# A hybrid decoder layer on one core: per-row roots and more products on TensorE in the opening, and a residual that the storing transfers add

## The chip, the core and the metric

The kernel runs on one core of a Trainium2 chip. Five engines work beside each other: TensorE (PE; its weight loads are listed as PEld) makes products into PSUM, VectorE (DVE), ScalarE (ACT) and GpSimd (POOL) work elementwise, and SyncE (SP) mostly issues transfers; POOL and ACT issue some as well. Every engine takes its instructions strictly in the order in which they stand in its own queue. The metric is the time of one execution in microseconds (us), lower is better; the median of three runs stands for a kernel.

## What is computed

One decoder layer on x (1024 x 1024, float32) with a conditioning vector c (1024):

```python
c_act = jax.nn.silu(c)
mod = c_act @ w_ada[l] + b_ada[l]
sh1, sc1, g1, sh2, sc2, g2 = [m[:, None, :] for m in jnp.split(mod, N_MOD, axis=-1)]
h = rmsnorm(x, pre_w_mix[l]) * (1.0 + sc1) + sh1
proj = h @ w_in[l]
...
mix = jnp.concatenate([attn, rec], axis=-1) @ w_out[l]
x = x + g1 * rmsnorm(mix, post_w_mix[l])
h = rmsnorm(x, pre_w_mlp[l]) * (1.0 + sc2) + sh2
u = jnp.square(jax.nn.relu(h @ w_up[l]))
x = x + g2 * rmsnorm(u @ w_down[l], post_w_mlp[l])
```

`rmsnorm(x, w)` divides each row by the root of its mean square plus 1e-6 and multiplies by w. The change touches the two ends: the first line of `h` (norm of x, shift `sh1`, scale `sc1`) with the first products of `h @ w_in`, and the last line, the final residual.

## The kernel before

The 1024 rows of x are eight tiles of 128 rows (`tb` 0 to 7) in two halves of four tiles (`th` 0 and 1); the 1024 columns are eight blocks of 128 (`kb` 0 to 7) and, in memory, two halves of 512 (`half`, `hf`). For precision a product is made of a high and a low part of each operand (`h`/`l` at a name's end), hence three products where the mathematics has one.

**The order** is the order of the code. From the line `pin(True, ACT, DVE, POOL, PE)` on, `Queue` keeps every instruction behind the last one on its engine, so the order in which lambdas and helpers are called is the order in the queues. All recorded operations have the one line L39, so tiles' names tell them apart.

**The opening** (about 0 to 70 us). SP loads x for tiles 0 to 3, then the weights `w_ada` of the first shift and scale as tiles `wa<gate>_<qt>_<kp>` (gate 0 is the shift, 1 the scale; `qt` is a quarter of the columns), with the weights `wqr`, `wkvr` between them. ACT squares each half row (`norm_sq`, tile `jx`). `norm_rstd(th)` takes the four rows' sums together: one POOL sum (`ssum`), one POOL `tensor_scalar` (`t_x`), one POOL power -0.5 (`r_x`). `norm_scale` multiplies x by it. `first_T` transposes a block of four x tiles on TensorE (`xT`), and `split_evac` makes of it `hhi` (ACT), `f` (POOL) and `hlo` (DVE), with the column's factors `a1`, `sh1`, `ns1`.

These factors come from the first modulation. For kb 0 and 1 (`qt` 0), `mod0_cols(e)` makes the shift as eight products of a 128x128 weight tile with a column of `cs` (silu of c), 128x1 each, while the scale's eight tiles are first summed on DVE (`mod0_acc`, tile `m`) and then reduced by one product with a column of ones. For kb 2 to 7 (`qt` 1 to 3) shift tiles are scaled on ACT and summed on POOL (`mod1_shift`), scale tiles are summed on DVE (`mod1_scale`), and `mod1_cols(qt)` reduces both by products with ones: eight for `qt` 1, four for `qt` 2 and 3, for which DVE first folds the two halves of the shift's sum (`wa<-wa`, 128x256). `mod1_finish` turns the columns into `a1`, `sh1`, `ns1` on DVE. Each float32 128x1 product stands in the trace as two records.

The loop over kb issues the products `pq` (512 wide, weights `wq`) and `pk` (256 wide, weights `wkv`) of four tiles with `hhi`, then the transpose of the next block and the modulation's columns, then the products with `hlo`.

**The middle** is not touched except for one store: `out_proj(tb)` computes x after the first sub-layer (`xr`) and stores it by a POOL transfer to a scratch array `x1d`.

**The tail.** The last group of the down projection adds products to `acc<tb>_<half>`, and a list `later` places the last norm's steps behind the products: `square` (ACT), `root` (DVE and POOL, tile `rrf`), `gated` (POOL, times the gate `gw`), `scaled` (ACT, times the root), `residual` (DVE, plus x1 loaded from `x1d` through `take()`), and a store by SP. Rows 2 and 6 end in `final`, one DVE instruction for root and residual together. `last_rows` does rows 3 and 7: the last products are `pdlx`, row 7's gated halves are `gl`, its root `l_r`; row 3 is scaled on ACT and its x1 added on POOL.

## Time and profile before

| | us |
|---|---|
| runs (three) | 1121.09, 1121.69, 1123.86 |
| median | 1121.69 |
| the profiled execution | 1118.99 |
| its span | 1117.2 |
| TensorE busy in it | 1073.3 |

The profiled execution is one more execution with its own time; its span is the time between its first and last recorded instruction, and the rest, 1.8 us, lies around it. The views read below are the page (busy times, the chain that ended last, transfers), the list of waits, the timeline of stretches, and windows of 2 us.

### The profile page before, as it was taken

The numbers are of one execution on the slowest core, as the hardware profiler recorded it, in microseconds if no ns is written. First come the engines' busy times: TensorE is split into PE (matmuls) and PEld (weight loads), VectorE is DVE, ScalarE is ACT, GpSimd is POOL, SyncE is SP. The second block draws the span as 40 slices with busy tenths as digits, with TensorE's granted clock in tenths as the row PEclk, the third lists the DMA queues.
The fourth block names the chain that finished last, engine by engine and source line by source line (L and its number), as shares of the span: only waits on it lengthen the run. The fifth ranks groups of instructions, "written<-read, shape, count | busy, mean of one in ns | idle before, by whom it ended". The sixth has DMA issues, their size and how long they took to land.

```text
span 1117.2 us, 16056 instructions
## 1 busy us (share of the span) xinstructions
PE 1073.3 (96%) x5406; PEld 878.0 (79%) x5406; DVE 817.6 (73%) x1338; ACT 593.7 (53%) x1228; POOL 404.4 (36%) x522
## 2 busy tenths in 40 slices
PE   5899999999999999999999999999999999999984
PEld 4788676788788788888888888888888888888863
DVE  4965877878865664639777766767767787998777
ACT  5645554374465664565655555556664544555343
POOL 3644211034224753422434434443333334300046
PEclk9999999999999999999999999999999999999997
DMA  9601400634310343323577676767998888987554
GB/s 354 243 11 38 133 1 22 196 97 139 126 58 1 118 156 113 115 74 121 198 247 252 230 258 230 255 216 248 324 348 297 274 287 279 334 283 244 160 179 160
DMA packets 103699, 207.30 MB, mean 186 GB/s; under 512 B 13344, under 2 KB 14000, under 8 KB 103616
## 3 DMA queue, kind: packets, MB, share of 16 engines
q1 hardware_dynamic: 89568, 161.07, 42.4%
q0 software_dynamic: 13760, 44.68, 12.0%
q8 instruction: 42, 0.69, 0.3%
q10 hardware_dynamic: 288, 0.52, 0.1%
q14 instruction: 41, 0.34, 0.1%
HBM read 151.17 MB, written 55.05 MB: 185 GB/s over the span
## 4 chain that ended last, share of the span: by engine, by line
PE 79%; DVE 7%; ACT 4%; DMA 4%; POOL 3%; issue 2%; SPq 0%; DVEq 0%; POOLq 0%; ACTq 0%
PE pua L39 14%; PE pda L39 13%; PE pdc L39 7%; PE puc L39 7%; PE po L39 6%; PE pu L39 4%; PE pdb L39 3%; PE pub L39 3%; PE pv L39 3%; PE phg L39 3%; PE phq L39 3%; PE phf L39 3%; PE pq L39 3%; DVE acc L39 2%; DMA wa<-wada 1%
## 5 line engine op out<-in xcount | busy, mean ns | idle before, releaser
L39 POOL TENSOR_TENSOR b<-b,b 128x512 f32<-128x512 f32 x64 | 90.0, 1406 | 221.7 <-DMA b<-w_dn 221.3
L39 ACT ACTIVATE s<-s 128x512 f32<-128x512 f32 x84 | 52.9, 631 | 32.5 <-DVE s L39 31.1
L39 ACT ACTIVATE dw<-dwr 128x512 fp32r<-128x512 f32 x72 | 45.3, 630 | 44.9 <-DMA dwr<-td 26.5
L39 DVE TENSOR_TENSOR dw<-dwr,dw 128x512 fp32r<-128x512 f32 x72 | 57.5, 799 | 9.0 <-ACT dw L39 8.9
L39 DVE TENSOR_TENSOR acc<-pda,acc 128x512 f32<-128x512 f32 x68 | 46.3, 682 | 12.3 <-PE pda L39 12.2
L39 POOL DMA_DIRECT2D td<-b x64 | 35.9, 561 | 19.0 <-POOL b L39 19.0
L39 DVE TENSOR_TENSOR wt<-s,wt 128x512 fp32r<-128x512 f32 x42 | 38.8, 924 | 1.2 <-ACT wt L39 1.1
L39 ACT ACTIVATE s<-pua 128x512 f32<-128x512 f32 x28 | 16.7, 596 | 39.6 <-PE pua L39 36.9
L39 ACT ACT_TABLE_LOAD x28 | 35.9, 1283 | 1.2 <-PEq L1704 0.7
L39 POOL DMA_DIRECT2D b<-w_dn x64 | 34.4, 540 | 2.6 <-issue 2.5
L39 DVE SCALAR_TENSOR_TENSOR macc<-wada,cs,macc 128x512 f32<-128x512 f32 x42 | 33.6, 799 | 2.2 <-DMA wada<-wada 1.6
L39 POOL TENSOR_TENSOR comb<-comb,rd 128x512 f32<-128x512 f32 x8 | 11.7, 1458 | 63.3 <-DVE rd L39 44.2
L39 PE MATMUL pua<-bt_0h,wt 128*128 128x512 f32 x84 | 32.7, 389 | 0.0
L39 PE MATMUL pua<-bt_1h,wt 128*128 128x512 f32 x84 | 32.7, 389 | 0.0
L39 PE MATMUL pua<-bt_2h,wt 128*128 128x512 f32 x84 | 32.7, 389 | 0.0
L39 PE MATMUL pua<-bt_3h,wt 128*128 128x512 f32 x84 | 32.7, 389 | 0.0
L39 DVE TENSOR_TENSOR wt<-a,wt 128x512 fp32r<-128x512 f32 x42 | 32.7, 777 | 0.0
L39 ACT ACTIVATE wt<-s 128x512 fp32r<-128x512 f32 x42 | 26.3, 627 | 10.1 <-DVE s L39 9.8
L39 POOL TENSOR_TENSOR acc<-acc,gw 128x512 f32<-128x512 f32 x14 | 20.2, 1454 | 30.6 <-ACT fin L39 30.6
L39 PE MATMUL pda<-dw,du_6h 128*128 128x512 f32 x96 | 29.8, 392 | 1.1 <-DVE acc L39 1.1
L39 PE MATMUL pdc<-dw,du_3h 128*128 128x512 f32 x96 | 29.7, 390 | 0.2 <-DVE acc L39 0.2
L39 DVE TENSOR_TENSOR s<-puc,s 128x512 f32<-128x512 f32 x14 | 9.7, 690 | 27.3 <-issue 25.2
(754 smaller groups left out, 3796.6 us busy)
## 6 DMA issues: line engine op xcount, KB each, us to landing
dur<-ud SPq DMA_DIRECT2D x112, 256.0 KB, 4.4
wada<-wada SPq DMA_DIRECT2D x64, 256.0 KB, 3.4
b<-w_dn POOLq DMA_DIRECT2D x64, 256.0 KB, 5.1
td<-b POOLq DMA_DIRECT2D x64, 256.0 KB, 3.3
dwr<-td SPq DMA_DIRECT2D x64, 256.0 KB, 4.2
a<-w_u SPq DMA_DIRECT2D x56, 256.0 KB, 4.5
dwr<-w_dn SPq DMA_DIRECT2D x48, 256.0 KB, 4.5
ud<-s SPq DMA_DIRECT2D x42, 256.0 KB, 3.4
```

Of the source, the lines that this page charges most:

```text
L39: ins = op(*args, **kw)
```

## The change

It has three parts.

**Opening.** (1) `norm_rstd(th, a, b)` takes rows a to b: one small DVE instruction for each row and one POOL power for the group, and is called for rows 0 and 1, then 2, then 3 as their squares are there; the factor 32 of the mean moves into `prew1s`. Rows 0 and 1 are then scaled on DVE, 2 and 3 on ACT. (2) ACT runs a sigmoid on a constant first, and silu of c comes behind the first row's squares. (3) For kb 0 and 1 the scale's tiles 4 to 7 are no longer summed on DVE but multiplied with `cs` on TensorE, four 128x1 products more in each `mod0_cols`; the scale's tile `wa1_0_0` is loaded ahead of the shift's `wa0_0_0`. (4) For `qt` 1 the last two blocks of both gates go to TensorE too, eight products more in `mod1_cols(1)`; for `qt` 3 the DVE fold is left out and `mod1_cols(3)` makes eight products where it made four. (5) Calls of `mod1_shift`, `mod1_scale`, the low part of `wq` (now `first_wql`), the second half's scaling of x and the squares of the second four tiles stand at other kb. (6) At kb 0 all `pq` products stand ahead of the `pk` products.

**Middle.** `out_proj` stores x of six of the eight row tiles straight into `out`; only rows 3 and 7 go to `x1d`.

**Tail.** For rows 0, 4, 1, 5, 2 and 6 there is no x1 load, no DVE residual and no SP store: both halves are scaled on ACT, and POOL issues two transfers which add the tile onto `out` (`onto_x`). Their second gated half is made on DVE. Rows 3 and 7 end in one DVE instruction for each half, with root and x1, and a store on SP and ACT in turn.

```diff
-    def norm_rstd(th):
-        ss = small.tile([P, 4], F32, tag="ss4", bufs=1, name=f"ssum{th}")
-        POOL.tensor_tensor(ss, ssx[th][:, :, 0], ssx[th][:, :, 1], ALU.add)
-        rx[th] = rstd_of(ss, D, 4, f"x{th}")
+    def norm_rstd(th, a, b):
+
+        if not a:
+            rx[th] = small.tile([P, 4], F32, tag="rr4", name=f"r_x{th}")
+        t = small.tile([P, 4], F32, tag="rs4", name=f"t_x{th}{a}")
+        for i in range(a, b):
+            DVE.tensor_scalar(t[:, i:i + 1], ssx[th][:, i, 0:1], ssx[th][:, i, 1:2], D * EPS, ALU.add, ALU.add)
+        POOL.tensor_tensor(rx[th][:, a:b], t[:, a:b], mhalf[:, a:b], ALU.pow)
...
         for k in range(KB):
-            wsh = wa1[0, 2 * e + k // 4, 0][:, k % 4 * P:k % 4 * P + P]
-            PE.matmul(pst[:, 0:1], lhsT=wsh, rhs=cs[:, k:k + 1], start=(k == 0), stop=(k == KB - 1))
+            PE.matmul(pst[:, 0:1], lhsT=wa0(e, k, 0), rhs=cs[:, k:k + 1], start=(k == 0), stop=(k == KB - 1))
+        for k in range(4, KB):
+            PE.matmul(pst[:, 1:2], lhsT=wa0(e, k, 1), rhs=cs[:, k:k + 1], start=(k == 4), stop=False)
         if between:
             between()
-        PE.matmul(pst[:, 1:2], lhsT=acc, rhs=ones[:, 0:1], start=True, stop=True)
+        PE.matmul(pst[:, 1:2], lhsT=acc, rhs=ones[:, 0:1], start=False, stop=True)
...
-        if kps[-1] == 3 and qt > 1:
+        if kps[-1] == 3 and qt == 2:
             w0 = wa1[qt, 0, 0]
             DVE.tensor_tensor(w0[:, 0:256], w0[:, 0:256], w0[:, 256:512], ALU.add)
...
         pst = a_ps(f"pm1_{qt}")
-        n = 2 if qt == 1 else 1
+        n = 2 if qt in (1, 3) else 1
         for j in range(4):
+            for h in range(2 if qt == 1 else 0):
+                PE.matmul(pst[:, j:j + 1], lhsT=wa1[1, 3, j // 2][:, 256 * h + (j % 2) * P:256 * h + (j % 2 + 1) * P],
+                          rhs=cs[:, 6 + h:7 + h], start=(h == 0), stop=False)
...
-            for gate in (0, 1) if qt == 0 else (1, 0):
+            for gate in (0, 1) if qt == 0 and kp % 2 else (1, 0):
...
+        if kb == 1:
+            mod1_shift(1, (1, 2))
+            mod1_scale(1, (2,))
...
         if kb == 0:
-            mod1_shift(1)
-        if kb == 1:
-            mod1_scale(1, range(2, 4))
+            mod1_shift(1, (0,))
         if kb in (2, 4):
-            mod1_shift(kb // 2 + 1, range(2, 4))
+            mod1_shift(kb // 2 + 1, range(kb - 2, 4))
             mod1_scale(kb // 2 + 1, range(2, 4))
...
-            nc.gpsimd.dma_start(x1d[tb][:, hs], xr)
+            nc.gpsimd.dma_start(x1d[tb // 4][:, hs] if tb % 4 == 3 else out[tb * P:(tb + 1) * P, hs], xr)
...
-    def residual(tb, half):
-        DVE.tensor_tensor(accs[tb][half], accs[tb][half], take(), ALU.add)
-        pend.append((out[tb * P:(tb + 1) * P, half * 512:half * 512 + 512], accs[tb][half]))
+    def onto_x(tb):
+
+        for half in range(2):
+            POOL.dma_start(out[tb * P:(tb + 1) * P, half * 512:half * 512 + 512], accs[tb][half], accum_op=ALU.add)
...
-                on(step + 2, lambda tb=tb, half=half: gated(tb, half))
-                for j, hf in ((3, 1 - half), (4, half)) if t < 2 else ():
-                    on(step + j, lambda tb=tb, hf=hf: scaled(tb, hf))
-                for j, hf in ((4, 0), (5, 1)) if t < 2 else ():
-                    on(step + j, lambda tb=tb, hf=hf: residual(tb, hf))
+                on(step + 2, lambda tb=tb, half=half: gated(tb, half, DVE))
+                for hf in (1 - half, half):
+                    on(step + 3, lambda tb=tb, hf=hf: scaled(tb, hf))
+                on(step + 4, lambda tb=tb: onto_x(tb))
...
-        final(6, 1)
-        xa = [take(), take()]
-        for half in range(2):
-            scaled(a, half)
-            POOL.tensor_tensor(accs[a][half], accs[a][half], xa[half], ALU.add)
-        for half in range(2):
-            DVE.scalar_tensor_tensor(gl[half], gl[half], one["r"][:, 0:1], take(), ALU.mult, ALU.add)
-            (nc.scalar if half else nc.sync).dma_start(out[b * P:(b + 1) * P, h[half]], gl[half])
-        store(a, 0)
-        final(6, 0)
-        store(a, 1, nc.scalar)
+        for tb, rr, src in ((a, rr_[a], accs[a]), (b, one["r"], gl)):
+            for half in range(2):
+                DVE.scalar_tensor_tensor(src[half], src[half], rr[:, 0:1], take(), ALU.mult, ALU.add)
+                (nc.scalar if half else nc.sync).dma_start(out[tb * P:(tb + 1) * P, h[half]], src[half])
```

TensorE's queue at the very start, before the change. `pm` is the bank of the first column's shift and scale, `wa_0_0` and `wa_0_1` weight tiles (quarter and block of rows, then a buffer's number, which tells the two gates apart), `m` the sum made on DVE; x4 is four 128x1 products.

```order
L39 MATMUL pm_0_265<-cs,wa_0_0_144 128x1 x4
L39 MATMUL pm_0_265<-cs,wa_0_1_148 128x1 x4
L39 MATMUL xT_0_274<-c_ident,x_0_93 128x128
L39 MATMUL xT_0_274<-c_ident,x_0_132 128x128
L39 MATMUL xT_0_274<-c_ident,x_0_136 128x128
L39 MATMUL xT_0_274<-c_ident,x_0_140 128x128
L39 MATMUL pm_0_265<-ones,m_0_254 128x1
L39 MATMUL pq_285<-wq0h,hhi_0_291 128x512
L39 MATMUL pq_285<-wq0l,hhi_0_291 128x512
L39 MATMUL pk_303<-wkv0h,hhi_0_291 128x256
L39 MATMUL pk_303<-wkv0l,hhi_0_291 128x256
```

And after the change:

```order
L39 MATMUL pm_0_270<-cs,wa_0_0_146 128x1 x4
L39 MATMUL pm_0_270<-cs,wa_0_1_148 128x1 x4
L39 MATMUL pm_0_270<-cs,wa_0_1_150 128x1 x4
L39 MATMUL xT_0_283<-c_ident,x_0_93 128x128
L39 MATMUL xT_0_283<-c_ident,x_0_132 128x128
L39 MATMUL xT_0_283<-c_ident,x_0_136 128x128
L39 MATMUL xT_0_283<-c_ident,x_0_140 128x128
L39 MATMUL pm_0_270<-ones,m_0_265 128x1
L39 MATMUL pq_294<-wq0h,hhi_0_300 128x512
L39 MATMUL pq_294<-wq0l,hhi_0_300 128x512
L39 MATMUL pq_295<-wq0h,hhi_0_300 128x512
L39 MATMUL pq_295<-wq0l,hhi_0_300 128x512
```

A third group of four products stands ahead of the transposes, and the `pk` products no longer stand behind the first two `pq` products.

GpSimd's queue at the end, before the change. `acc_0_8030` and `acc_0_8675` are the last halves of rows 2 and 6, `acc_0_8062` and `acc_1_8289` row 3, `l_r` the root of row 7.

```order
L39 TENSOR_TENSOR acc_0_8030<-acc_0_8030,gw_5216 128x512
L39 TENSOR_TENSOR rrf_10925<-ssf_10924,mhalf 128x1
L39 TENSOR_TENSOR acc_0_8675<-acc_0_8675,gw_5216 128x512
L39 TENSOR_TENSOR acc_0_8062<-acc_0_8062,gw_5216 128x512
L39 TENSOR_TENSOR rrf_10964<-ssf_10963,mhalf 128x1
L39 TENSOR_TENSOR acc_1_8289<-acc_1_8289,gw_5216 128x512
L39 TENSOR_TENSOR l_r<-l_part,mhalf 128x1
L39 TENSOR_TENSOR acc_0_8062<-acc_0_8062,x_3_0_10857 128x512
L39 TENSOR_TENSOR acc_1_8289<-acc_1_8289,x_3_1_10872 128x512
```

And after it, where `acc_0_8078` and `acc_1_8305` are row 3, and `acc_0_8691` and `acc_1_8159` row 6:

```order
L39 DMA out<-acc_0_8046 128x512
L39 DMA out<-acc_1_8263 128x512
L39 TENSOR_TENSOR rrf_10917<-ssf_10916,mhalf 128x1
L39 TENSOR_TENSOR acc_0_8078<-acc_0_8078,gw_5232 128x512
L39 TENSOR_TENSOR rrf_10950<-ssf_10949,mhalf 128x1
L39 TENSOR_TENSOR acc_1_8305<-acc_1_8305,gw_5232 128x512
L39 DMA out<-acc_0_8691 128x512
L39 DMA out<-acc_1_8159 128x512
L39 TENSOR_TENSOR l_r<-l_part,mhalf 128x1
```

The two additions of x to row 3 behind `l_r` are gone, two gated halves have moved to VectorE, and two issues of transfers onto `out` for row 6 now stand between row 3's last gated half and `l_r`.

## Rows read from the trace of the kernel before

**Rows 1.** The page: the first row is the busy time of each engine, its share of the span and its instructions; the second the chain that ended last, by engine.

```profile
PE 1073.3 (96%) x5406; PEld 878.0 (79%) x5406; DVE 817.6 (73%) x1338; ACT 593.7 (53%) x1228; POOL 404.4 (36%) x522
...
PE 79%; DVE 7%; ACT 4%; DMA 4%; POOL 3%; issue 2%; SPq 0%; DVEq 0%; POOLq 0%; ACTq 0%
```

**Rows 2.** The view of waits, first 70 us: engine and what waits, what it waits for, then us in total, times, and the longest.

```profile
PE pm L39 <- DMA wa<-wada: 10.7, 1, 10.7
...
PE pm L39 <- DVE hlo L39: 1.7, 1, 1.7
...
PE pk L39 <- POOL wkv0l L39: 0.6, 1, 0.6
```

**Rows 3.** The timeline, 9.5 to 19.6 us: start us, us, engine, line, operation, out<-in, count, and in brackets the idle time before it and what ended that. A row with a count spans all of its instructions.

```profile
10.68 3.55 PE L39 MATMUL pm<-cs,wa 128*128 128x1 f32 x16 [10.68 <-DMA wa<-wada]
...
11.37 0.28 DVE L39 TENSOR_SCALAR m<-wa,cs 128x128 f32<-128x128 f32 x1 [6.38 <-DMA wa<-wada]
...
14.09 1.09 PE L39 MATMUL xT<-c_ident,x 128*128 128x128 f32 x4
...
16.85 0.79 PE L39 MATMUL pq<-wq0h,hhi 128*128 128x512 f32 x1 [1.30 <-ACT hhi L39]
```

**Rows 4.** The timeline of TensorE, 19.2 to 38.6 us, columns as in rows 3.

```profile
19.70 0.63 PE L39 MATMUL pq<-wq0l,hhi 128*128 128x512 f32 x1
...
23.96 2.23 PE L39 MATMUL pm<-cs,wa 128*128 128x1 f32 x16
...
29.23 0.40 PE L39 MATMUL pq<-wq1h,hhi 128*128 128x512 f32 x1
...
31.06 0.95 PE L39 MATMUL pm<-ones,wa 128*128 128x1 f32 x8
32.89 1.23 PE L39 MATMUL pm<-ones,m 128*128 128x1 f32 x8 [0.88 <-DVE m L39]
...
37.12 0.63 PE L39 MATMUL pq<-wq2h,hhi 128*128 128x512 f32 x1
```

**Rows 5.** The windows of the stretch 22 to 40 us, 2 us each, of which three are shown: the stretch, its length, busy time (and instructions) of PE, PEld, DVE, ACT and POOL, the granted clock of TensorE, the DMA share, GB/s.

```profile
34.00:36.00 2.00, 2.00 (x11) 1.77 (x11) 1.74 (x8) 1.37 (x3) 0.50 (x1) 0.75 1.05 396
36.00:38.00 2.00, 2.00 (x8) 1.61 (x7) 2.00 (x3) 1.52 (x4) 1.58 (x2) 0.50 1.06 406
38.00:40.00 2.00, 2.00 (x13) 1.82 (x12) 2.00 (x2) 0.00 (x0) 1.76 (x2) 0.90 1.04 391
```

**Rows 6.** The timeline, 44 to 57 us, columns as in rows 3.

```profile
44.92 0.60 PE L39 MATMUL pm<-ones,wa 128*128 128x1 f32 x4
...
45.39 0.58 PE L39 MATMUL pm<-ones,m 128*128 128x1 f32 x4
...
53.73 1.50 DVE L39 TENSOR_TENSOR wa<-wa 128x256 f32<-128x256 f32 x1
...
55.95 0.60 PE L39 MATMUL pm<-ones,wa 128*128 128x1 f32 x4 [1.74 <-DVE hlo L39]
```

**Rows 7.** The view of waits of TensorE, 1050 to 1104 us, columns as in rows 2.

```profile
PE pda L39 <- DVE acc L39: 2.6, 4, 1.2
```

**Rows 8.** The timeline of VectorE, 1089 to 1097.5 us, columns as in rows 3: two of the eight residual additions.

```profile
1090.61 0.68 DVE L39 TENSOR_TENSOR acc<-acc,x 128x512 f32<-128x512 f32 x1
...
1094.77 1.18 DVE L39 TENSOR_TENSOR acc<-acc,x 128x512 f32<-128x512 f32 x1
```

**Rows 9.** The timeline, 1098 us to the end, columns as in rows 3.

```profile
1099.34 0.79 DVE L39 SCALAR_TENSOR_TENSOR acc<-acc,rrf,x 128x512 f32<-128x512 f32 x1
...
1100.50 2.96 POOL L39 TENSOR_TENSOR acc<-acc,gw 128x512 f32<-128x512 f32 x2
...
1100.95 0.28 PE L39 MATMUL pdlx<-dw,du_4l 128*128 128x256 f32 x1
...
1102.26 1.27 DVE L39 TENSOR_TENSOR acc<-pda,acc 128x512 f32<-128x512 f32 x2
...
1103.64 0.75 DVE L39 TENSOR_TENSOR acc<-pdlx,acc 128x256 f32<-128x256 f32 x2
...
1104.31 1.80 POOL L39 TENSOR_TENSOR acc<-acc,gw 128x512 f32<-128x512 f32 x1
...
1105.03 1.63 DVE L39 TENSOR_TENSOR gl<-acc,gw 128x512 f32<-128x512 f32 x1
...
1106.65 0.74 DVE L39 SCALAR_TENSOR_TENSOR acc<-acc,rrf,x 128x512 f32<-128x512 f32 x1
1106.81 0.99 POOL L39 TENSOR_TENSOR l_r<-l_part,mhalf 128x1 f32<-128x1 f32 x1 [0.69 <-DVE l_part L39]
...
1111.17 0.74 DVE L39 SCALAR_TENSOR_TENSOR acc<-acc,rrf,x 128x512 f32<-128x512 f32 x1
1111.28 0.34 ACTq L1638 DMA_DIRECT2D out<-gl  x1
```

**Rows 10.** The page: a row of the costliest groups (line, engine, operation, count | busy us, mean ns of one | idle before), and two of the DMA issues (count, KB each, median us from issue to landing).

```profile
L39 POOL DMA_DIRECT2D td<-b x64 | 35.9, 561 | 19.0 <-POOL b L39 19.0
...
b<-w_dn POOLq DMA_DIRECT2D x64, 256.0 KB, 5.1
td<-b POOLq DMA_DIRECT2D x64, 256.0 KB, 3.3
```

**Rows 11.** The DMA issues of 1040 to 1118 us, columns as in the last rows of rows 10.

```profile
out<-acc SPq DMA_DIRECT2D x13, 256.0 KB, 2.4
```

More of the change, by code (lines that the diff above doesn't have):

```diff
@@ L304, in mod1_scale @@
                 w2 = wa1[qt, kp, 1][:, 256 * k2:256 * k2 + 256]
-                part = acc[:, 256 * k2:256 * k2 + 256] if qt == 1 else acc[:, 0:256]
-                if kp == 0 and (k2 == 0 or qt == 1):
+                part = acc[:, 256 * k2:256 * k2 + 256] if qt in (1, 3) else acc[:, 0:256]
+                if kp == 0 and (k2 == 0 or qt in (1, 3)):
                     DVE.tensor_scalar(part, w2, cs[:, k:k + 1], None, ALU.mult)
@@ L336, in hybrid_layer @@
     pin(True, ACT, DVE, POOL, PE)
-    for tb in range(4):
-        norm_sq(tb)
-    norm_rstd(0)
-    norm_scale(0, 0, ACT, (0, 1))
-    mod0_acc(0, {k: lambda k=k: norm_scale(0, 0, DVE, (k - 2,)) for k in (4, 5)})
+    norm_sq(0)
+    silu_c()
+    norm_sq(1)
+    norm_rstd(0, 0, 2)
+    norm_scale(0, 0, DVE, (0, 1))
+    norm_sq(2)
+    norm_rstd(0, 2, 3)
+    norm_sq(3)
+    norm_rstd(0, 3, 4)
+    norm_scale(0, 0, ACT, (2, 3))
+    mod0_acc(0)
     xT0 = []
@@ L349, in first_kv, with first_mm @@
         wkv.extend([(hi[:, 0:256], lo[:, 0:256]), (hi[:, 256:512], lo[:, 256:512])])
-    def first_mm(kb, tb, part):
+    def first_mm(kb, tb, part, which=(0, 1)):
         sl = slice(tb * P, tb * P + P)
         ah, al = (h[:, sl] for h in hh[kb][0])
-        for pst, (bh, bl), first, last in ((pq0[tb], wq[kb], True, True),
-                                           (pk0[tb], wkv[kb], tb % 2 == 0, tb % 2 == 1)):
+        for w in which:
+            pst, (bh, bl), first, last = ((pk0[tb], wkv[kb], tb % 2 == 0, tb % 2 == 1) if w else
+                                          (pq0[tb], wq[kb], True, True))
             if part == 0:
@@ L362, in first_wq, with first_wql @@
     def first_wq(kb):
-        wq.append(load_split(g_, f"wq{kb}", I["w_q"][kb], raw=wqr[kb]))
+        hi, lo = (g_(f"wq{kb}{n}", dt=F32R) for n in "hl")
+        ACT.activation(hi, wqr[kb], AF.Copy)
+        wq.append((hi, lo))
+    def first_wql(kb):
+        hi, lo = wq[kb]
+        DVE.tensor_tensor(lo, wqr[kb], hi.bitcast(F32), ALU.subtract)
     first_wq(0)
+    first_wql(0)
     for kb in range(KB):
@@ L392, in hybrid_layer @@
             pin(False, SP)
-        first_mm(kb, 0, 0)
-        first_mm(kb, 1, 0)
-        if kb == 5:
-            mod1_cols((kb + 1) // 2)
-        first_mm(kb, 2, 0)
-        first_mm(kb, 3, 0)
+        for which in ((0,), (1,)) if kb == 0 else ((0, 1),):
+            first_mm(kb, 0, 0, which)
+            first_mm(kb, 1, 0, which)
+            if kb == 5:
+                mod1_cols((kb + 1) // 2)
+                first_wql(kb + 1)
+            first_mm(kb, 2, 0, which)
+            first_mm(kb, 3, 0, which)
         if kb + 1 < KB:
@@ L1518, in square, with gated @@
         ACT.activation(a_ps(f"fin{tb}_{half}"), accs[tb][half], AF.Square, accum_out=ssr[tb][:, half:half + 1])
[L1520 to L1521 removed]
+    def gated(tb, half, eng=POOL):
+        eng.tensor_tensor(accs[tb][half], accs[tb][half], gw2[:, half * 512:half * 512 + 512], ALU.mult)
     def root_of(r, part, a, b):
@@ L1589, in add @@
             DVE.tensor_tensor(dst, pst, dst, ALU.add)
-        xs = {}
-        def final(tb, half):
-            if (tb, 0) not in xs:
-                xs[tb, 0], xs[tb, 1] = take(), take()
-            DVE.scalar_tensor_tensor(accs[tb][half], accs[tb][half], rr_[tb][:, 0:1], xs[tb, half], ALU.mult, ALU.add)
-            store(tb, half)
         dmm(bb, g, 2, t, True)
@@ L1621, in last_rows @@
         gated(a, 1)
-        assert not later
         for i in range(2):
@@ L1625, in last_rows @@
             sq(acp[i], ss[:, 1 + i:2 + i], 256)
+        for step in range(nstep + 3, max(later) + 1):
+            rest(step)
         DVE.tensor_tensor(gl[1], accs[b][1], gw2[:, h[1]], ALU.mult)
```

67 lines of the change are left out of this document (35 added, 32 removed).

## The prediction

> **What bounds the kernel now.** I read the page first: TensorE is busy for 96% of the span and makes up 79% of the chain that ended last [rows 1]. So a us taken from another engine counts only where TensorE waits for it, and a us put on TensorE counts nearly whole. The change works at the two ends, where that is least true, so I went to the waits and the timelines there.
>
> In the opening TensorE waits 10.7 us for the first weights, which nothing here shortens, then 1.7 us once for `hlo` and 0.6 us for `wkv0l` [rows 2]; 0.88 us for `m` stands in the timeline [rows 4]. All that the change could take away there is about 3.2 us; what it adds are 128x1 products on the engine that is the bound. Their price depends on the clock. A 128x512 product took 0.63 us at 19.70 and 0.40 at 29.23 [rows 4]; it took 0.63 again at 37.12, and there the windows show a granted clock of 0.50 [rows 5], which is 1.2 GHz of 2.4. By its duration the clock is at the half up to about 23 us.
>
> At the end TensorE's last product ends at 1100.95 + 0.28 = 1101.23. The last elementwise work ends at 1111.17 + 0.74 = 1111.91, and the span at 1117.2, 5.3 us after the store that follows it is issued [rows 9]. So over 10 us of last norm stand behind the last product, on DVE and POOL, whose instructions stretch each other: two products of `pdlx` take 0.75, but a lone `gl` takes 1.63 beside POOL's `gated` of 1.80 [rows 9], and a residual addition takes 0.68 or 1.18 [rows 8].
>
> **Opening, first column.** Sixteen records of eight products take 3.55 us, 0.222 each [rows 3]. Four more products are eight more records: +1.78. They are on the path: the transposes follow at 14.09 and the first `pq` at 16.85, which waits 1.30 for `hhi` [rows 3], and `hhi` waits for these columns. The shift's first tile now lands second; DVE's first use of the second tile comes 11.37 - 10.68 = 0.69 later [rows 3], so +0.69. The roots per row and the shorter `m` make x and the sum ready earlier, but TensorE is not ready for them: with 24 records it comes to the transposes at about 11.4 + 5.3 = 16.7 instead of 14.2. I cost them at nothing; their cover is these products, and without it the best they could return is the time that the products add. In return `pk` no longer stands ahead of `pq`: -0.6 [rows 2]. Sum +1.9, at half clock. If the clock rises at the same moment as before, 1.9 us of half-speed work are made up at double speed, and only 0.95 is lost; if it rises later with the work, all is lost. No row of before decides; I take the middle, so -0.5. The Trainium skill ("TensorE: Matmul & The Clock Gate", What's actually happening) says that the moment of the rise does not follow the kernel's start and varies between runs; by that the loss would be the smaller one in some executions, and no run here shows it yet.
>
> **Second column** (`mod0_cols(1)`). 2.23 us for 16 records is 0.139 each [rows 4]; eight more: +1.1.
>
> **Quarter 1** (`mod1_cols(1)`). Eight more products are 16 records at 0.95 / 8 = 0.12 [rows 4]: +1.9. DVE and ACT lose the last blocks, so the 0.88 us wait for `m` goes [rows 4]: -0.9. Sum +1.0.
>
> **Quarter 2.** Here all four shift blocks are now scaled and summed in one stretch of kb 2, before only half. A wait for them is not in the trace; the nearest rows are no wait at 44.92 and the 1.74 before 55.95 [rows 6]. So 0 to 1.7, nothing below zero since TensorE does not wait there now. I take 0.4, near the row of the same place.
>
> **Quarter 3.** Four more products, eight records at 0.60 / 4 = 0.15 [rows 6]: +1.2. The fold of 1.50 on DVE, ahead of the `hlo` for which TensorE waits 1.74 [rows 6], goes: -1.5. Sum -0.3. Moved squares and scalings of the second four tiles stay under the products of kb 5 to 7; were that cover gone, the transposes of the second half would wait, up to the same 1.7.
>
> Opening: 1.9 - 0.5 + 1.1 + 1.0 + 0.4 - 0.3 = **+3.6**, bounds +1 and +6.
>
> **Middle.** The stores of x1 keep number, size and queue, only their address changes: nothing. TensorE-bound work behind the opening shifts as a whole.
>
> **Last group.** TensorE waits 2.6 us for DVE's additions into `acc` [rows 7]. DVE loses eight residual additions of 0.68 to 1.18 [rows 8] and gains six gated halves, for which the uncontended row is 0.68 too; POOL loses six and gains twelve issues at 0.56 [rows 10]. A gated half may still come ahead of an addition that TensorE wants. I take -0.6, bounds -1.5 and +0.5.
>
> **Tail**, against the last product at 1101.23 (everything relative to it). DVE no longer has the two `final` of row 2 (0.79 alone in the row shown [rows 9]) but one gated half of row 6, so the additions that began at 1102.26 begin at about 1100.8 and those of `pdlx` end at about 1102.9, not 1104.4 [rows 9]. POOL: the root of row 6 ends near 1100.5, row 3's first gated half at 1102.0 (2.96 / 2 each [rows 9]), its root by 1102.9, the second half by 1104.5 at the contended 1.80 [rows 9]. Then come two issues of 0.56 [rows 10], to 1105.6, and `l_r` behind them, 0.99 [rows 9], to 1106.6. DVE ends `gl` near 1105.0 (two, one at 0.68 and one at the contended 1.63), row 3's two halves by 1106.5 and row 7's by 1108.1 to 1108.4, at 0.74 each with POOL silent [rows 9]. Before it was 1111.91: **-3.5**, bounds -2 and -5. What waits for the queued issues is `l_r` alone: had ACT's scaling of row 6 been late, `l_r` would be too.
>
> The adding transfers have no row here. Their cover is the last plain store, issued at 1108.4 and landing 2.4 later [rows 11], at 1110.8; row 6's last one is issued at 1105.1 and so has 5.7 us. Plain POOL transfers of this size land after 3.3 or 5.1 us [rows 10]; both are inside, and I take 5.1, since work is added. Row 3's and 7's stores start alone, so nothing else is late. The Trainium skill ("DMA: Bandwidth & Descriptors", Rules for kernel authors) says that an accumulating transfer reads its destination and writes it later. Taken as two trips of its fitted 2.0 us plus bytes / 436e3 that is an estimate of 5.2 us, still inside; no run here shows it so far.
>
> **Sum.** 3.6 - 0.6 - 3.5 = -0.5. The profiled execution took 1118.99, so it becomes 1118.5; the median of the runs lies 2.7 above the profiled execution, so I give 1121.2 for the median. A measurement of this kernel can tell about 0.3% (3.4 us) from no change.
>
> **Rivals.**
>
> *The clock repays the opening.* The windows grant 0.75 in 34 to 36, 0.50 in 36 to 38 and 0.90 in 38 to 40: at half for 1.0 + 2.0 + 0.4 = 3.4 us, right behind the products with ones and the 0.88 us wait [rows 4, 5]. If that wait's end, and TensorE's longer unbroken start, take this stretch away, its 3.4 us return 1.7, and the rise at the same moment another 0.5: opening +1.4, with the tail at -4.5 and -0.9 for the last group a total of -4.0, 1117.7. For it: TensorE idles less. Against it: the stretch stands right behind 128x1 products, of which there will be twice as many.
>
> *A second half-clock stretch.* `mod0_cols(1)` grows to 24 records, some 3.3 us, as long as the stretch 31.06 to 34.1 that came ahead of the fall [rows 4]. If the clock falls there too, and longer after `mod1_cols(1)`, each such stretch costs 1.7: net -0.5 + 1.7 = +1.2, 1122.9, and with two and the 1.7 wait in quarter 2, +4.2, 1125.9. For it: the fall in the trace. Against it: the present 2.23 us of such products brought none.
>
> *The adding transfer ends last* (slower). Place: row 6's second transfer, issued at 1105.1. It decides from 5.7 us on; beyond that each us is paid in full. At 6.6 (twice 3.3) the cost is 0.9, net +0.4, 1122.1; at 10.2 (twice 5.1) it is 4.5, net +4.0, 1125.7. For it: read and write for each byte. Against: the queue is nearly empty there.
>
> *The change does not do what it says:* the roots per row bring nothing, as said; that is in the forecast.
>
> **Chances.** Forecast 0.48; clock repays 0.25; second stretch 0.16; adding transfer last 0.11. The first leaves part of its spread beyond 3.4 us on either side (0.06 and 0.04); of the second case nearly all is faster (0.22), of the third and fourth about half slower (0.15). So faster 0.28, same 0.53, slower 0.19. Range 1115.8 to 1125.8: low end opening +1, last group -1.5, tail -5; high end the two slower mechanisms at their worst.
>
> **What would show it.** First `pq` at 19.0 to 19.5 instead of 16.85, no wait of `pk` for `wkv0l`, none for `m` at `mod1_cols(1)`, the first transposes of the second half some 3.6 us later; a granted clock of 0.50 or not in 34 to 40; the last store issued 7 us after the last product instead of 10.7; transfers onto `out` landing within 5.7 us. I am wrong if the first `pq` comes before 18, if TensorE is not what ends the first column, or if the last event is a transfer issued by POOL.

## The result and the profile after

| | before | after |
|---|---|---|
| median of six runs, us | 1121.39 | 1126.65 |
| the six runs, us | 1120.09 to 1123.86 | 1124.93 to 1129.74 |
| ratio, 95% interval | | 1.0046 [1.0026, 1.0065] |
| the profiled execution, us | 1118.99 | 1125.87 |
| its span, us | 1117.2 | 1124.1 |
| last product ends, us | 1101.23 | 1111.11 |
| from there to the end of the span, us | 15.97 | 12.99 |

The change makes the kernel 5.3 us slower; 1121.2 was predicted, 1125.8 was the upper end. The two last lines divide it: behind the last product 3.0 us are gained, and before it 9.9 are lost in this pair of executions.

The page after, busy times and chain, against [rows 1]: TensorE has 40 instructions and 8.3 us more, and POOL's share of the chain has come up from 3 to 4%.

```profile
PE 1081.6 (96%) x5446; PEld 886.4 (79%) x5446; DVE 806.2 (72%) x1330; ACT 594.6 (53%) x1231; POOL 402.3 (36%) x523
...
PE 79%; DVE 8%; POOL 4%; ACT 4%; issue 3%; DMA 2%; SPq 0%; DVEq 0%; POOLq 0%; ACTq 0%
```

TensorE's timeline in the opening, against [rows 3, 4, 6] (a row with a count spans all its instructions):

```profile
12.15 5.25 PE L39 MATMUL pm<-cs,wa 128*128 128x1 f32 x24 [12.15 <-DMA wa<-wada]
...
19.88 0.80 PE L39 MATMUL pq<-wq0h,hhi 128*128 128x512 f32 x1 [1.30 <-ACT hhi L39]
...
25.11 0.60 PE L39 MATMUL xT<-c_ident,x 128*128 128x128 f32 x4
25.55 2.74 PE L39 MATMUL pm<-cs,wa 128*128 128x1 f32 x24
...
28.37 0.72 PE L39 MATMUL pq<-wq0h,hlo 128*128 128x512 f32 x1
...
49.76 0.60 PE L39 MATMUL pm<-ones,wa 128*128 128x1 f32 x4 [0.50 <-DVE hlo L39]
...
60.83 1.05 PE L39 MATMUL pm<-ones,wa 128*128 128x1 f32 x8 [1.75 <-DVE hlo L39]
...
70.31 0.60 PE L39 MATMUL xT<-c_ident,x 128*128 128x128 f32 x4
```

The same timeline of before, at block 1 and block 7:

```profile
23.11 1.06 PE L39 MATMUL xT<-c_ident,x 128*128 128x128 f32 x4
...
26.27 0.48 PE L39 MATMUL pq<-wq0h,hlo 128*128 128x512 f32 x1
...
62.98 0.60 PE L39 MATMUL xT<-c_ident,x 128*128 128x128 f32 x4
```

Read against the same instructions of before: the first `pm` is 1.47 later, the first `pq` 3.03 (16.85 before), the transposes of block 1 2.00. From then on the shift should only grow by what the change adds. It grows to 5.46 at the transposes of block 5 (55.67, 50.21 before) and to 7.33 at those of block 7.

The windows (columns as in [rows 5], the granted clock third from the end):

```profile
28.00:30.00 2.00, 2.00 (x10) 1.81 (x10) 1.45 (x7) 1.02 (x2) 0.14 (x1) 0.61 1.06 408
30.00:32.00 2.00, 2.00 (x8) 1.61 (x8) 2.00 (x5) 2.00 (x6) 2.00 (x2) 0.54 1.05 403
38.00:40.00 2.00, 2.00 (x10) 1.75 (x10) 1.66 (x7) 1.24 (x3) 0.37 (x1) 0.67 1.04 391
40.00:42.00 2.00, 2.00 (x7) 1.70 (x7) 1.93 (x5) 2.00 (x7) 0.88 (x2) 0.50 1.01 368
62.00:64.00 2.00, 2.00 (x11) 1.81 (x12) 1.03 (x5) 0.00 (x0) 0.00 (x0) 0.64 0.01 2
64.00:66.00 2.00, 2.00 (x9) 1.81 (x9) 0.00 (x0) 0.00 (x0) 0.00 (x0) 0.50 0.00 0
298.00:300.00 2.00, 2.00 (x12) 2.00 (x11) 1.89 (x6) 1.96 (x5) 0.00 (x0) 0.52 0.00 0
```

In [rows 5] one stretch of 3.4 us at 0.50 stands, at 35.0 to 38.4. Now there are three in the opening: 28.4 to 31.9, behind the second column's 24 records; 38.7 to 42.1, behind quarter 1's; 62.6 to 66.0, behind quarter 3's. A fourth stands at 298 to 302, where nothing was changed and before had none. Each lasts 3.4 us with TensorE busy throughout, and so costs 1.7.

One execution doesn't tell how general that is: the traces of early_only and no_extra, two kernels further down that have none of the added products, show 10.2 us at half clock in the opening too. A run's mean clock c gives its time at half clock as 2 x (1 - c) x span (up to the clock's first fall the windows print 1.00 whatever the products take, so the half clock of the start isn't in it). With the tail of before it is 21.2 us for before (mean of 23 runs) and 25.9 for the new opening (6 runs of `new_opening`, below); with the new tail 19.2 for the old opening (12 runs of `new_tail`) and 25.9 for after (6). Only kernels with one tail can be compared so, since most of this time lies behind the last product, where it costs nothing: in the trace of before 13.7 of 17.9 us, by this window.

```profile
1101.23:1117.20 15.97, 0.00 (x0) 0.00 (x0) 10.23 (x14) 3.39 (x10) 8.44 (x7) 0.57 0.33 127
```

So the new opening adds 4.7 to 6.7 us at half clock, with a standard error of some 1.5. Where TensorE is busy in all of it, that costs 2.4 to 3.4. It is an upper reading: from run to run of one kernel, a us more at half clock goes with 0.28 us more time (all kernels here pooled), not with 0.5.

The end: TensorE's waits of 1050 to 1112 us (columns as in [rows 2], against [rows 7]), the timeline from 1108.5, and the transfers onto `out` (against [rows 11]).

```profile
PE pda L39 <- DVE acc L39: 1.8, 4, 0.8
```

```profile
1110.83 0.28 PE L39 MATMUL pdlx<-dw,du_4l 128*128 128x256 f32 x1
...
1113.28 2.12 POOL L39 DMA_DIRECT2D out<-acc  x2
...
1114.93 1.40 DVE L39 SCALAR_TENSOR_TENSOR acc<-acc,rrf,x 128x512 f32<-128x512 f32 x2
1115.09 1.00 POOL L39 TENSOR_TENSOR l_r<-l_part,mhalf 128x1 f32<-128x1 f32 x1
...
1116.26 1.40 DVE L39 SCALAR_TENSOR_TENSOR gl<-gl,l_r,x 128x512 f32<-128x512 f32 x2
...
1117.69 0.34 ACTq L1660 DMA_DIRECT2D out<-gl  x1
```

```profile
out<-acc POOLq DMA_DIRECT2D x12, 256.0 KB, 4.7
...
out<-gl SPq DMA_DIRECT2D x1, 256.0 KB, 4.5
out<-gl ACTq DMA_DIRECT2D x1, 256.0 KB, 4.0
```

The last store is issued 6.6 us after the last product (1117.69 against 1111.11; 10.7 before), and lands in 4.0 to 4.5 instead of 2.4. An adding transfer takes 4.7 in the median of twelve, row 6's two 4.2 and 6.1. Issuing one holds POOL for 1.06 in the row shown (2.12 for two) and for 0.89 to 0.95 in the other five pairs, not for 0.56.

### The profile page after: what moved, and what is told of

Its sections match the earlier page's. It is cut to its first block, busy times and chain, and to the rows that moved or that the text cites. A ratio compares the mean times of both kernels' runs of the same rounds, so it can differ in the third digit from the quotient of the medians.

```text
span 1124.1 us, 16081 instructions
## 1 busy us (share of the span) xinstructions
PE 1081.6 (96%) x5446; PEld 886.4 (79%) x5446; DVE 806.2 (72%) x1330; ACT 594.6 (53%) x1231; POOL 402.3 (36%) x523
## 4 chain that ended last, share of the span: by engine, by line
PE 79%; DVE 8%; POOL 4%; ACT 4%; issue 3%; DMA 2%; SPq 0%; DVEq 0%; POOLq 0%; ACTq 0%
PE pua L39 14%; PE pda L39 13%; PE pdc L39 7%; PE puc L39 7%; PE po L39 6%; PE pu L39 4%; PE pdb L39 3%; PE pub L39 3%; PE pq L39 3%; PE pv L39 3%; PE phg L39 2%; PE phq L39 2%; PE phf L39 2%; PE pk L39 1%; PE pm L39 1%
## 5 line engine op out<-in xcount | busy, mean ns | idle before, releaser
L39 DVE TENSOR_TENSOR dw<-dwr,dw 128x512 fp32r<-128x512 f32 x72 | 52.5, 730 | 5.9 <-ACT dw L39 5.9
L39 DVE TENSOR_TENSOR wt<-s,wt 128x512 fp32r<-128x512 f32 x42 | 34.9, 832 | 1.0 <-ACT wt L39 0.9
L39 DVE TENSOR_TENSOR acc<-pdc,acc 128x512 f32<-128x512 f32 x36 | 24.6, 683 | 8.4 <-PE pdc L39 8.3
L39 ACT ACTIVATE hhi<-xT,sh,a 128x512 fp32r<-128x512 f32 x16 | 12.1, 780 | 34.6 <-PE xT L39 14.9
```

The costliest lines, as they stand in the source:

```text
L39: ins = op(*args, **kw)
```

## The experiments

Each was timed in five rounds beside the kernel before on the same chip. A number behind the label is the ratio to before with its interval; 0.001 is 1.1 us. In the expectations, the clock theory says that the added narrow products bring further half-clock stretches, the work theory that only the time of the moved work counts.

**The two ends apart.** `new_tail` is the opening of before with the changed middle and tail, `new_opening` the opposite.

```diff
# new_tail: lines ahead of proj3 from before, the rest from after
# new_opening: lines ahead of proj3 from after, the rest from before
```

> The kernel before with only the middle and the tail of the change (x1 stored into the output, adding transfers, rows 3 and 7 as one instruction a half). Both theories: the tail is worth what the profile after shows, 12.99 us from the last product to the span's end instead of 15.97, so 3.0 us, and 0.8 us less waiting in the last group: 1117.5 to 1118.5 against 1121.4, and one half-clock stretch in the opening as before.

> The changed opening alone, with the tail of the kernel before. Clock theory and work theory alike: the opening costs 7 to 9 us, 1128 to 1131. If the sum of this and of the tail alone is not the whole change (5 us slower), the two parts meet somewhere.

new_tail 0.9975 [0.9963, 0.9986], new_opening 1.0060 [1.0047, 1.0073]. The tail gains 2.8 us (between 1.6 and 4.1) and the opening loses 6.7 to 8.0 (the second is 1.0046 - 0.9975). The two add up to 1.0035, inside the interval of after. All of the loss is the opening's.

**The added products.** `no_extra` is after without its 20 products of 128x1 (the sums and the fold are back on VectorE, the loads in the old order); `spread` keeps them and puts them one or two at a time between the 512-wide products of the same block.

```diff
# no_extra
-        for k in range(4):
+        for k in range(KB):
...
-        for k in range(4, KB):
-            PE.matmul(pst[:, 1:2], lhsT=wa0(e, k, 1), rhs=cs[:, k:k + 1], start=(k == 4), stop=False)
...
-        if kps[-1] == 3 and qt == 2:
+        if kps[-1] == 3 and qt > 1:
...
# spread
                 PE.matmul(pst, lhsT=ah, rhs=bl, start=False, stop=False)
+                if kb or w or tb > 1:
+                    some(1 if kb == 1 else 2)
```

> The changed kernel without any of the added 128x1 products (40 records fewer: the sums go back to VectorE, the fold is back), everything else of the opening and the tail as changed. Clock theory: both further half-clock stretches go with the products, 1.7 us each, beside the products' own 5 to 6 us: 1117 to 1119 with one stretch left. Work theory: the products' own time goes, some 5 us less the waits that come back (up to 2.4 us), the stretches stay: 1121 to 1124 with three stretches.

> The changed kernel with the same 128x1 products, but those of the second column, the eight new ones of quarter 1 and all of quarter 3 placed one or two at a time between the wide products of the same kb instead of in a row. Clock theory: the stretch behind 28 us goes and perhaps the later two, 1.7 us each: 1.7 to 5 us under the changed kernel, 1122 to 1125. Work theory: the number of products is the same, so within 1 us of the changed kernel, 1126 to 1127, with as many stretches.

no_extra 1.0006 [0.9996, 1.0016]: the products cost 0.0040, 4.5 us. What stays against new_tail, 0.0031 or 3.5 us, is not products. The time is what the work theory expected, and the clock theory, which had one stretch left, missed: windows of 2 us give 6.8 us at half clock from 33.6 on and 3.4 from 60.9, as much as in after. By the mean clock no_extra is at 23.3 us (12 runs), 2.6 under after and 4.1 over new_tail. TensorE's timeline of no_extra shows waits for sums at the places to which they were moved; two of its windows follow:

```profile
32.20 1.05 PE L39 MATMUL pm<-ones,wa 128*128 128x1 f32 x8 [1.95 <-POOL wa L39]
...
50.35 0.50 PE L39 MATMUL pq<-wq4l,hhi 128*128 128x512 f32 x1 [0.43 <-DVE wq4l L39]
...
55.09 0.50 PE L39 MATMUL pq<-wq4h,hlo 128*128 128x512 f32 x1 [1.48 <-DVE hlo L39]
```

```profile
36.00:38.00 2.00, 2.00 (x8) 1.71 (x8) 1.89 (x5) 2.00 (x5) 0.97 (x1) 0.50 1.05 406
...
62.00:64.00 2.00, 2.00 (x10) 1.81 (x9) 0.00 (x0) 0.00 (x0) 0.00 (x0) 0.50 0.00 0
```

The first of these waits belongs to a sum for quarter 1 that stands there by my choice of place, since after makes products of it; so the 3.5 can't be laid wholly to the change.

spread 1.0049 [1.0032, 1.0066]: no gain. I had thought that it is the unbroken row of narrow products that brings the clock down. That form of the theory fell. Spread's timeline of TensorE, where the clock rises only between 33 and 35.6 (some 24.7 before); this execution, at 1131.63, is the slowest of spread's six, so the late rise need not be the rule:

```profile
33.03 0.63 PE L39 MATMUL pq<-wq0h,hlo 128*128 128x512 f32 x1
...
35.61 0.39 PE L39 MATMUL pq<-wq1l,hhi 128*128 128x512 f32 x1
```

**Narrow against wide.** Idle products in before, results unused: `more_narrow` has 20 of 128x1 (8 in the second column, 8 in quarter 1, 4 in quarter 3), as many as the change adds; `more_wide` has 22 of 128x512 at the same places.

```diff
# more_narrow, at the head of mod0_cols(1), mod1_cols(1) and mod1_cols(3)
+        for k in range(n):
+            PE.matmul(pst[:, 8:9], lhsT=ident, rhs=cs[:, k:k + 1], start=(k == 0), stop=(k == n - 1))
# more_wide
+            PE.matmul(pst, lhsT=ones_r, rhs=wq[kb][0], start=(k == 0), stop=(k == n - 1))
```

> The kernel before with 20 idle 128x1 products put ahead of the columns of kb 1 (8), quarter 1 (8) and quarter 3 (4): 40 records, some 5.2 us of TensorE, whose sums nobody reads. Clock theory (TensorE's narrow products let the granted clock fall, whether in a row or not): own time 4.3 us beyond the 0.9 us wait that they fill, and one or two more half-clock stretches of 1.7 us: 6 to 8 us over the kernel before. Work theory: 4.3 us over it and no more stretches than it has.

> The same places, but 22 idle 128x512 products in place of the 20 narrow ones, the same 5.1 us of TensorE at full clock. Clock theory: wide products keep the clock up, so at most their own 4.2 us over the kernel before, and less where the half-clock stretch behind quarter 1 goes (1.7 us); well under the narrow kernel. Work theory: as the narrow kernel within 1 us.

more_narrow 1.0068 [1.0056, 1.0080], 29.3 us at half clock; more_wide 1.0057 [1.0042, 1.0073], 20.6 (before: 21.9, 17 runs beside them). The times are not told apart, and more_wide cost more than the 4.2 us that its clock theory allowed. The half-clock times do differ. TensorE's timeline of each, more_narrow first:

```profile
35.08 0.63 PE L39 MATMUL pq<-wq1l,hhi 128*128 128x512 f32 x1
...
36.30 0.39 PE L39 MATMUL pq<-wq1l,hhi 128*128 128x512 f32 x1
```

```profile
23.52 0.67 PE L39 MATMUL xT<-c_ident,x 128*128 128x128 f32 x4
23.94 2.30 PE L39 MATMUL pm<-wq0h,ones_r 128*128 128x512 f32 x9
26.09 1.84 PE L39 MATMUL pm<-cs,wa 128*128 128x1 f32 x16
```

In more_narrow a product takes 0.63 as late as 35.08 (in the slowest of its six executions, 1133.39); in more_wide the transposes of block 1 show the half clock ending at 23.5, and the sixteen records behind the wide ones take 1.84. Narrow: 40 records at 0.115 (1.84 / 16) are 4.6, and (29.3 - 21.9) / 2 = 3.7 of clock make 8.3, measured 7.6. Wide: 22 products at 0.256 (2.30 / 9) are 5.6, less 0.6 of clock make 5.0, measured 6.4. The sums differ by 3.3 and the times by 1.2, uncertain by 2, so that the clock's part in the time is reckoned and not shown. Still, products which move nothing off any engine cost as much as the whole new opening.

**Parts of the change undone or alone.** `old_mod0`, `old_q1` and `old_q3` are after with the added products of kb 0 and 1, of quarter 1, of quarter 3 taken back. `early_only` is new_tail with the roots per row, the silu and table load, and `pq` ahead of `pk`; `mod0_only` is that with the added products of kb 0 and 1 and their load order.

```diff
# old_q1
-            for h in range(2 if qt == 1 else 0):
...
-            mod1_shift(1, (1, 2))
-            mod1_scale(1, (2,))
+            mod1_shift(1, (1, 2, 3))
+            mod1_scale(1, (2, 3))
# old_q3, which also brings back the fold
-        n = 2 if qt in (1, 3) else 1
+        n = 2 if qt == 1 else 1
# mod0_only, against early_only (old_mod0 is the reverse, in after)
-            for gate in (0, 1) if qt == 0 else (1, 0):
+            for gate in (0, 1) if qt == 0 and kp % 2 else (1, 0):
```

> The changed kernel with the scale of kb 0 and 1 summed on VectorE again and the shift's first tile loaded first; the rest as changed. By the terms of the trace after: eight records at half clock 1.75, the slot 0.7 to 1.1 and eight records of kb 1 0.5 to 1.1 come back, unless VectorE's sum of eight is late: 2.5 to 3.5 us under the changed kernel if the clock does not matter, up to 5 if a stretch goes with them.

> The changed kernel without the eight products added for quarter 1 (the last blocks are scaled and summed on ScalarE, GpSimd and VectorE again). Work theory: 16 records at 0.13, so -2.1, and the waits for these sums come back, which were 2.0 and 0.4 us in the kernel without any added product: within 1 us of the changed kernel. Clock theory: a wait idles TensorE as well, so the stretch behind quarter 1 stays: also about the same.

> The changed kernel with quarter 3 as before: VectorE's fold is back, four 128x1 products instead of eight. My prediction's step (the fold is what the wait of 1.74 ends on): 0.3 us slower than the changed kernel, 1127. Work theory from the trace after, where that wait stayed at 1.75 with the fold gone: eight records, 1.0 us, go and the fold adds at most 1.5: within 1 us of it. Clock theory: a stretch less behind 62 us in some executions, 0 to 1.7 us faster.

> The new tail with the old opening, of which only this is changed: roots as the rows land, silu behind the first squares, the early table load, and the pq products ahead of the pk products at kb 0. No product is added and no sum is moved. My step (roots hidden, the 0.6 us wait for wkv0l gone): 0 to 0.6 us under the new tail alone, 1118.2 to 1118.8. If it is 2 us or more over it, this part costs something that no term of mine holds.

> The new tail with the early part (1118.2) and the added products of kb 0 and 1 in the changed order of loads; sums of the other quarters as before. If these products cost what they cost in the changed kernel: 2.6 us more, 1120 to 1121.5, and the remaining 5 us of the opening belong to the moved sums and quarter 3. If they cost 4 us or more here, the clock that they let fall is the larger part of the loss.

old_mod0 1.0023 [1.0011, 1.0035], old_q1 1.0046 [1.0028, 1.0063], old_q3 1.0029 [1.0017, 1.0041]: of after's 1.0046, 0.0023, nothing and 0.0017 go, the first barely told apart from after, the others not. All three together (no_extra) are. early_only 0.9974 [0.9962, 0.9985] is new_tail again: the roots as the rows land are worth nothing. From early_only to no_extra only the calls of point (5) of the opening's change move: 0.0032, 3.6 us, is what that costs there. mod0_only 0.9983 [0.9973, 0.9993] costs 0.0009 where its undoing in after gave 0.0023, neither far outside the noise. The parts don't add up; their half-clock times don't either. Of two kernels with the same tail, mod0_only has eight narrow products more and less half clock (17.9 us, early_only 21.2). In early_only's trace a stretch begins near 24.8, inside a wait of 1.51 us for `m` that mod0_only doesn't have. So a fall can follow a wait as well as narrow products:

```profile
25.93 0.59 PE L39 MATMUL pm<-ones,m 128*128 128x1 f32 x2 [1.51 <-DVE m L39]
```

```profile
24.00:26.00 2.00, 0.49 (x5) 0.40 (x4) 1.80 (x3) 0.00 (x0) 1.26 (x1) 0.70 1.05 406
```

**The clock at the start, set by hand.** `warm_tail` and `warm_after` are new_tail and after with 24 idle 128x512 products on constants at the very start, while TensorE waits for its first weights.

```diff
+    for k in range(24):
+        PE.matmul(wps, lhsT=ones_r, rhs=wide, start=(k == 0), stop=(k == 23))
```

> The kernel before's opening with the new tail, and 24 idle 128x512 products on constants at the very start, while TensorE waits for its first weights (10.7 us in the trace of before). Clock theory: the clock rises while nothing is lost, so the first column's records, the transposes and kb 0's products, 12 us of half clock up to 23, run at full clock at least in part: 3 to 6 us under the new tail alone (1118.8), 1113 to 1116. Work theory (the half clock of the opening is given and costs the same in all): no change beyond 0.5 us.

> The changed kernel with the same 24 idle products at the start. Clock theory: it gains as much as the kernel with the old opening or more, 4 to 7 us, to 1120 to 1123, and the gap between the openings (8 us) shrinks to the products' own time at full clock and the new waits, 4 to 5 us. Work theory: no change, 1126 to 1127.

warm_tail 0.9981 [0.9968, 0.9994], warm_after 0.9998 [0.9985, 1.0011]. The two openings are 0.0017 or 1.9 us apart when started at full clock, against 8.0. After gains 5.3 from it, as its clock theory had it; new_tail gains nothing, and there that theory missed (3 to 6 us). The windows of warm_tail show why: its clock falls again near 11.5, right behind the wait for the loads, and is at 0.50 through the first products with `hhi`. Warm_after's clock falls too, near 14.8, but only behind its first column. So the two are not compared at one clock, and the 1.9 is no price of the narrow products.

```profile
8.00:10.00 2.00, 0.90 (x4) 0.40 (x3) 0.00 (x0) 1.95 (x7) 0.00 (x0) 1.00 1.00 356
...
18.00:20.00 2.00, 1.39 (x5) 0.79 (x5) 1.96 (x4) 1.09 (x4) 1.09 (x1) 0.50 1.05 405
```

TensorE's timeline of warm_after has the first column's 24 records at the full clock, 2.81 against 5.25:

```profile
11.79 2.81 PE L39 MATMUL pm<-cs,wa 128*128 128x1 f32 x24 [1.36 <-DVE m L39]
```

**The tail's transfers.** `row6_plain` is new_tail with row 6 loaded, finished on DVE and stored plainly, like rows 3 and 7.

```diff
-    for tb in (3, 7):
+    for tb in (6, 3, 7):
...
-                on(step + 4, lambda tb=tb: onto_x(tb))
+                if tb != 6:
+                    on(step + 4, lambda tb=tb: onto_x(tb))
```

> The new tail with row 6 loaded, finished by VectorE and stored plainly as rows 3 and 7 are, so that the last adding transfers are issued some 10 us before the end. If adding transfers in flight slow the last plain stores (they landed after 4.0 to 4.5 us in the changed kernel, 2.1 to 2.4 before), the stores land after 2.1 to 2.6 again; VectorE has two instructions of 0.7 more on the path, so the time stays within 1 us of the new tail alone (1118.8). If the four stores slow each other, they still take 4 us and the kernel is 1.5 us slower.

row6_plain 0.9955 [0.9938, 0.9971]. The transfers of its last 80 us: with no adding transfer close ahead, the plain stores land in 2.0.

```profile
out<-acc POOLq DMA_DIRECT2D x10, 256.0 KB, 5.0
...
out<-acc SPq DMA_DIRECT2D x2, 256.0 KB, 2.0
...
out<-gl SPq DMA_DIRECT2D x1, 256.0 KB, 2.0
```

**A better kernel.** `best` is early_only with that tail. `keep_warm` is best with 30 idle wide products at the start, one between each two products of the first column, and five ahead of the first `pq`. `warm_mod0` adds to it the change's four products for kb 1 alone; in `warm_mod0_x` ACT also scales two rows of the second half of x.

```diff
# keep_warm, in mod0_cols(0)
             PE.matmul(pst[:, 0:1], lhsT=wsh, rhs=cs[:, k:k + 1], start=(k == 0), stop=(k == KB - 1))
+            idle(1 - e)
# warm_mod0
+        for k in range(4, KB if e else 4):
+            PE.matmul(pst[:, 1:2], lhsT=wsc, rhs=cs[:, k:k + 1], start=(k == 4), stop=False)
# warm_mod0_x
-            norm_scale(0, 1, DVE, (2, 3))
+            norm_scale(0, 1, ACT, (2, 3))
```

> The early part of the opening, and the new tail with row 6 finished plainly. Both were worth 0 to 0.6 and 2.1 us apart: 1116 to 1117, faster than both kernels.

> The same with idle 128x512 products at the start (30), one between each two products of the first column, and five where TensorE waits for the first hhi. Clock theory: the clock now holds through the first column, so kb 0's products, 6 us at half clock, take 3: 2 to 4 us under the kernel without them. If the clock falls all the same, the idle products delay the first column and it is 0 to 3 us slower.

> The kernel with the idle wide products (1117.1), and the change's four added 128x1 products for kb 1 alone, so that VectorE sums four tiles there instead of eight. Clock theory: the 3.07 us wait for that sum goes, 0.9 us of products come, and the half-clock stretch behind the wait may go too (3.4 us of 6.8): 2 to 5 us faster, 1112 to 1115. Work theory (these products cost what they cost in the changed kernel): 0 to 1 us slower.

> The same, with rows 2 and 3 of the second half of x scaled on ScalarE instead of VectorE, since the transposes of kb 4 waited 1.51 us for VectorE there. Both theories: that wait goes, 0 to 1.5 us under the kernel before it in this list, unless ScalarE is then late with hhi.

best 0.9962 [0.9950, 0.9974], keep_warm 0.9958 [0.9946, 0.9970], warm_mod0 0.9939 [0.9926, 0.9952], warm_mod0_x 0.9952 [0.9939, 0.9965]. With the clock held, keep_warm comes to the transposes of block 1 at 20.30, 1.73 ahead of best (22.03), and gives it back in a longer wait for `m` (0.88 in best); its expected 2 to 4 us didn't come. In warm_mod0 the change's own products take that wait away, and with them the half clock is not up but down (14.7 us, keep_warm 21.0). TensorE's timeline of each:

```profile
20.30 0.60 PE L39 MATMUL xT<-c_ident,x 128*128 128x128 f32 x4
20.74 1.84 PE L39 MATMUL pm<-cs,wa 128*128 128x1 f32 x16
25.65 0.58 PE L39 MATMUL pm<-ones,m 128*128 128x1 f32 x2 [3.07 <-DVE m L39]
```

```profile
20.07 0.60 PE L39 MATMUL xT<-c_ident,x 128*128 128x128 f32 x4
20.50 2.74 PE L39 MATMUL pm<-cs,wa 128*128 128x1 f32 x24
23.10 0.36 PE L39 MATMUL pm<-ones,m 128*128 128x1 f32 x2
```

warm_mod0 at 1114.12 us beats both kernels, by 0.6% and 1.1%. That it is better than keep_warm rests on the wait in the trace; the intervals overlap. The scaling on ACT gains nothing.

## Why the prediction was wrong, step by step

The forecast was -0.5 us and 5.3 came. Its two sums were +3.6 for the opening (measured 6.7 to 8.0) and -4.1 for the end (measured -2.8, between -1.6 and -4.1). So the opening makes 3.1 to 4.4 of the miss; that of the end, 1.3, is within the noise.

**The step that failed is the clock's term in the opening.** It stood at -0.5, for the rise alone, and the rise did what it says. It came near 25.0, against 24.7 before (not about 23: the transposes at 23.11 still took 1.06), and gave back 0.8: the shift is 2.00 at block 1 and 2.10 at the first `pq` with `hlo`, with 0.9 of new records between them. What was left out of the sum is the clock behind it. The rival "a second half-clock stretch" had the mechanism, its place and its price of 1.7 for each, and I gave it 0.16 against 0.25 for "the clock repays", on the ground that before's 16 records brought no fall. In place of the -0.5, two further stretches stand in the opening of the trace after, 3.4 us, and the runs' mean clocks give at most 2.4 to 3.4, an error of up to 2.9 to 3.9 in this one term. Without the clock the opening costs some 4.3 to 4.6, and my terms without it were 4.1.

**What makes the stretches stays open.** That rows of narrow products can is borne out by the half-clock times of more_narrow and more_wide (29.3 and 20.6 us), though their times are not told apart. In the changed kernel it is only part of it: without any added product no_extra keeps 4.1 of the 6.7 us, and mod0_only and warm_mod0 have narrow products more than their neighbours and less half clock. The rival is the waits that moved sums bring, as in early_only; no run changed waits alone. Divided by parts of the edit, the products cost 4.5 us, where their terms and the load's slot came to 4.3 (1.78 + 0.69 + 1.1 + 1.0 - 0.3). The moved calls cost 3.5 in no_extra, where my sum had 0.4; one wait of 1.95 there is of my own placing, so it may be less in after. The stretch at 298 has no cause that a run here shows; new_tail has one at 290.

The range was also drawn too narrow. The forecast's own bounds reach +4.5 (6 + 0.5 - 2), 1126.2, and the rival with two stretches 1125.9, but it ended at 1125.8; at the low end -5.5 is 1116.2 and not 1115.8.

**Terms of the opening that were mis-sized**, by the profiled execution. The slot of the swapped load: 1.47 for 0.69, though the first landing varies by as much between executions (10.67 to 11.56 with the old order, 11.17 to 12.58 with the new). First column: 1.70 for 1.78. Second: 0.9 for 1.1. Quarter 1: 3.6 from its first product to its last instead of 3.06 with the wait, so +0.6 for +1.0; the wait for `m` is gone, as said. Quarter 2: waits of 0.50 and, at the next block, 0.44 for 0.4. Quarter 3: +1.0 for the products (60.83 to 62.71, against 55.95 to 56.86), but the fold's -1.5 never came: the wait for `hlo` is 1.75 as before. VectorE's timeline has the sums directly ahead of `hlo`:

```profile
55.96 4.16 DVE L39 SCALAR_TENSOR_TENSOR m<-wa,cs,m 128x256 f32<-128x256 f32 x4
60.04 0.74 DVE L39 SCALAR_TENSOR_TENSOR hlo<-xT,a,f 128x512 fp32r<-128x512 f32 x1
```

Four sums take 4.16 there, 3.31 before, and they begin 5.5 later, as late as TensorE is. I took the fold's time off TensorE's wait without asking when the work ahead of it would start. That the sums stretch because POOL sums beside them is argued; no run moved them.

**Right:** the roots per row at nothing (early_only), no wait for `wkv0l`, no transfer of POOL as the last event, and nearly the first `pq`, 19.88 for 19.0 to 19.5. The adding transfer was inside its 5.7 us in the median (4.7), but one of row 6's two took 6.1. It didn't end last, since the last plain store was issued at 1117.69 and landed 4.0 later. The second half's first transposes came 7.3 later (74.95, 67.63 before), not 3.6. The moment of the rise: with one and the same opening it came near 24.7 in before, 23.9 in new_tail and 23.8 in row6_plain (block 1's transposes took 1.06 from 23.11, 0.80 from 23.50, 0.95 from 23.06), and the stretches stood at 35.0 in before and at 34.1, 58.0 and 290 in new_tail. So far the Trainium skill ("TensorE: Matmul & The Clock Gate", What's actually happening) is borne out: it is not bound to the kernel's start. The estimate of 5.2 us from the Trainium skill ("DMA: Bandwidth & Descriptors", Rules for kernel authors for the two trips, Anatomy of one DMA — SWDGE (gpsimd) path for the time of one) stands near the medians of 4.7 to 5.0 measured for an adding transfer.

**The end.** Last group: waits of 1.8 instead of 2.6, -0.8 for -0.6. Tail: -3.0 for -3.5. The elementwise work came out as reckoned, the last store issued 6.6 us after the last product where 7 was said. (For the additions the sum took 1.5 off; its rows, two `final` of 0.79 less a gated half of 0.68, give 0.9. They began 2.1 earlier.) The term left at nothing was that store's own landing, 2.4 in [rows 11] and now 4.0 to 4.5, behind row 6's adding transfers, although POOL's queue and theirs are two. In row6_plain, with none close ahead, the stores land in 2.0; in time it gains 0.0020 on new_tail and best 0.0012 on early_only, the same way twice and resolved in neither.
